# First tile of x on another queue, a warming matmul moved, and state-space groups stepped in pairs, in a hybrid decoder layer

## Chip, cores and metric

The kernel runs on one core of one Trainium2 chip. The time is device microseconds of one execution; the kernel before was run three times and has 1466.87 us as its median.

## The reference

One decoder layer on 256 tokens of width 2048, in float32. Cut to what matters here:

```python
u    = rmsnorm(x, norm_mix_pre)
proj = u @ w_in                       # columns: z | x, B, C | dt | q | k | v
xbc  = silu(causal_depthwise_conv(xbc, conv_w, conv_b))
dt   = softplus(dt_raw + dt_bias);  a = -exp(a_log)
# Mamba-2, 8 groups of 4 heads of 64, state 128, two chunks of 128 tokens:
y    = (cb * decay_in) @ xdt  +  exp(a_cs) * (C @ states)  +  d_skip * x
yg   = y * silu(z);  yg = yg * rsqrt(mean(yg * yg, over the group) + EPS)
y_ssm = yg * ssm_norm_w
# 16 heads of dilated attention, three dilations mixed by softmax
h = x + rmsnorm(concat(y_ssm, y_att) @ w_out)
h = h + rmsnorm(relu(rmsnorm(h) @ w_up)**2 @ w_down)
```

Nearly all of the work is in the four products with `w_in`, `w_out`, `w_up` and `w_down`.

## The kernel before

Every weight is split into two parts, `hi` and `lo` (ScalarE rounds `hi` from the loaded tile `raw`, line 144; VectorE takes `lo = raw - hi`, line 145), and so are the activations (`ua`, `ub`, `uc` hold u; `sh`, `sl` and others what follows). A product is the sum of three of the four part products. A step is one tile of 256 rows by 512 columns of a weight: one load (line 158, from SP's queue, four `raw` buffers), one `hi`, one `lo` (five buffers each) and 16 or 12 matmuls. A block of 512 columns has eight steps. `gemm_features` (lines 468 and 471) gives a block with features on the partitions, `gemm_tokens` (`row_tile`, lines 323 to 325) one with tokens on the partitions.

The state-space part runs block by block: for each half, a features block for B and one for C, then twice a features block for x (`conv_block`, with the convolution on VectorE, lines 735 and 737) and a tokens block for the gate z (`gate_block`). Each x block holds two groups. Their own small work is a generator, `ssd_group`, that stands in the queue `waiting`. After each step of a block, `pump` takes the generator at the head, lets it write its program up to the next `yield` and puts it back at the end. So the small matmuls of the groups lie between the steps of later blocks, and with two groups waiting they take turns. The parts of a group are, by what TensorE does:

- line 752: the group's rows of `acs` are loaded into `bc` on ScalarE's queue (two buffers); lines 757 to 768: C times B, and transposes of B and x;
- lines 784 to 786: decays in `bc` (VectorE, and exp on ScalarE); line 789: the state (`st`);
- line 793: C times the state, which becomes `yo` (line 795); line 801: the decays in `bc` times x, 8 small matmuls; then `yg` (804, 806), its squares (810, ScalarE), their mean `rm` (138), the inverse root `gr` (139, GpSimd) and the scaling (814);
- line 821: four transposes of `yg`, split into `sh` and `sl`.

The small products go to PSUM tiles `ps`, of which there are two. Within an engine the order is set by a scheduler from the order and the priorities in which the program is written; weights have priority (`high_priority`), and an engine then takes its instructions strictly in that order.

The first block (`first_block`, priority and order by hand) loads x and the first weights in turn on SP's queue, while TensorE does matmuls of ones (`warm`), the transpose of the norm's weight `pre` and the transposes of the first tile of x (`turn_x`, line 549).

Of the kernel before, what the change touches and what calls it, by code (L numbers as in the profile page):

```python
# [44 lines left out]
BUFS = 5  # L45
RAWS = 4
LAG_DOWN = 3
WARM = 6
STAY = 4
SUMS = 10  # L50
FINE = 6
FIRST = 3
UP_SEVENS = (1, 3, 4, 6)
V_SEVENS = (1, 3, 5, 6)
QK_SEVENS = (1, 3, 5)
# [22 lines left out]
def hymba_layer(ctx: ExitStack, tc: tile.TileContext, x, norm_mix_pre, w_in, conv_w, conv_b, dt_bias, a_log,  # L78
                d_skip, ssm_norm_w, w_out, norm_mix_post, norm_mlp_pre, w_up, w_down, norm_mlp_post,
                consts, out):  # L80
    nc = tc.nc
    w_in, w_out, w_up, w_down = w_in[0], w_out[0], w_up[0], w_down[0]
    xt = x[0].rearrange("(t p) d -> p t d", p=P)
# [48 lines left out]
    def psmall():  # L132
        return psm.tile([P, NB], F32, name="ps")
# [170 lines left out]
    waiting = deque()  # L304
# [213 lines left out]
        for _ in range(n):  # L518
            nc.tensor.matmul(p[:, 0:P], ones, ones, start=True, stop=True)

    def load_x(k0):
        cs = slice(k0 * P, (k0 + KB) * P)
        nc.sync.dma_start(xs0[:, :, cs], xt[:, :, cs])

    def load_parameters():
        for r, src in enumerate((norm_mlp_pre, ssm_norm_w)):
# [16 lines left out]
    def turn_x(k0):  # L543

        q = [psmall() for _ in range(KB)] if k0 % (2 * KB) else spare
        for f in range(KB):
            for t in range(NT):
                ks = slice((k0 + f) * P, (k0 + f + 1) * P)
                nc.tensor.transpose(q[f][:, t * P:(t + 1) * P], xs0[:, t, ks], ident)
        return q  # L550
# [9 lines left out]
    def first_block():  # L560
        acc = features()
        raws = {}

        def load(k0):
            raws[k0] = fetch(w_in, k0, COL_B, step=1 if k0 < FINE else KB)

        def part(k0, hi, lo, js):
            split(hi[:, js], lo[:, js], raws[k0][:, js])

        load_x(0)  # L570
        load(0)
        load_x(KB)
        load(KB)
        p = psmall()
        nc.tensor.transpose(p[:, 0:16], pre, ident[0:16, 0:16])
        nc.vector.tensor_copy(w_pre, p[:, 0:16])
        q = turn_x(0)
        warm(STAY)
        hi, lo = parts()
        for f in range(KB):  # L580
            split_x(0, q, f)
            part(0, hi, lo, slice(f, f + 1))
        for k0 in range(0, NK, KB):
            k1, k2 = k0 + KB, k0 + 2 * KB
            if k2 < NK:
                load_x(k2)
                load(k2)
            elif k2 == NK:
                load_parameters()
            products(acc, hi, lo, k0, [(f, 0) for f in range(4)])  # L590
            if k1 < NK:
                q = turn_x(k1)
            products(acc, hi, lo, k0, [(f, 1) for f in range(4)])
            if k1 == NK:
                break
            hi, lo = parts()
            if k1 >= FINE:
                part(k1, hi, lo, slice(0, KB))
            for f in range(KB):
                behind[:] = split_x(k1, q, f)  # L600
                if k1 < FINE:
                    part(k1, hi, lo, slice(f, f + 1))
            if k0 >= 4:
                squares(k0 // KB - 2)
        return acc

    nc.scalar.activation(rstd, half[:, 0:NT], AF.Copy)
    with tc.high_priority(offset=2 * AHEAD), tc.manual_schedule():
        nc.sync.dma_start(ident, consts[:, 0:P])
        nc.scalar.dma_start(pre, norm_mix_pre[0].rearrange("(k p) -> k p", p=P))  # L610
        warm(WARM)
        first = first_block()
# [135 lines left out]
    def ssd_group(sp, g, bT, cT, xT, z):  # L748

        hs = slice(HPG * g, HPG * (g + 1))  # L750
        bc = sp.tile([P, HPG, S], F32, name="bc")
        nc.scalar.dma_start(bc, acs_d[hs].partition_broadcast(P))

        p = psmall()
        for c in range(NT):
            cs = slice(c * P, (c + 1) * P)
            nc.tensor.matmul(p[:, cs], bT[:, cs], cT[:, cs], start=True, stop=True)
        nc.tensor.transpose(p[:, S:S + P], bT[:, 0:P], ident)
        cbm = sp.tile([P, NT, P], F32, name="cbm")
        nc.vector.tensor_tensor(cbm, p[:, :S].rearrange("p (c i) -> p c i", c=NT),  # L760
                                triu[:, None, :].to_broadcast([P, NT, P]), op=ALU.mult)
        bn = sp.tile([P, P], F32, name="bn")
        nc.vector.tensor_copy(bn, p[:, S:S + P])

        p = psmall().rearrange("p (c f) -> p c f", c=NT)
        for c in range(NT):
            for f in range(2):
                nc.tensor.transpose(p[:, c, f * P:(f + 1) * P], xT[:, f, c * P:(c + 1) * P], ident)
        xs = sp.tile([P, NT, HPG, HD], F32, name="xs")
        nc.scalar.activation(xs.rearrange("p c r d -> p c (r d)"), p, AF.Copy)  # L770
        xdt = sp.tile([P, NT, HPG, HD], F32, name="xdt")
        for c in range(NT):
            nc.vector.tensor_tensor(xdt[:, c], xs[:, c], dt[:, c, hs, None].to_broadcast([P, HPG, HD]), op=ALU.mult)
        xdd = sp.tile([P, HPG, HD], F32, name="xdd")
        nc.gpsimd.tensor_tensor(xdd, xdt[:, 0], toend[:, hs, None].to_broadcast([P, HPG, HD]), op=ALU.mult)
        for c in range(NT):
            nc.gpsimd.tensor_tensor(xs[:, c], xs[:, c], skip_b[:, hs, None].to_broadcast([P, HPG, HD]), op=ALU.mult)
        yield

        for c in range(NT):  # L780
            m = bc[:, :, c * P:(c + 1) * P]
            for r in range(HPG):
                h = HPG * g + r
                nc.vector.tensor_scalar(m[:, r], m[:, r], acs[:, c, h:h + 1], 0.0, op0=ALU.subtract, op1=ALU.min)
            nc.scalar.activation(m, m, AF.Exp)
            nc.vector.tensor_tensor(m, m, cbm[:, c, None, :].to_broadcast([P, HPG, P]), op=ALU.mult)

        p = psmall()
        nc.tensor.matmul(p[:, :S], bn, xdd.rearrange("p r d -> p (r d)"), start=True, stop=True)
        st = sp.tile([P, HPG * HD], F32, name="st")  # L790
        nc.vector.tensor_copy(st, p[:, :S])
        yield
        nc.tensor.matmul(p[:, S:], cT[:, P:], st, start=True, stop=True)
        yo = sp.tile([P, HPG, HD], F32, name="yo")
        nc.vector.tensor_tensor(yo, p[:, S:].rearrange("p (r d) -> p r d", r=HPG),
                                eacs[:, hs, None].to_broadcast([P, HPG, HD]), op=ALU.mult)
        nc.gpsimd.tensor_tensor(xs[:, 1], xs[:, 1], yo, op=ALU.add)
        p = psmall().rearrange("p (c r d) -> p c r d", c=NT, r=HPG)
        for c in range(NT):
            for r in range(HPG):  # L800
                nc.tensor.matmul(p[:, c, r], bc[:, r, c * P:(c + 1) * P], xdt[:, c, r], start=True, stop=True)

        yg = sp.tile([P, NT, HPG * HD], F32, name="yg")
        nc.vector.tensor_tensor(yg, p.rearrange("p c r d -> p c (r d)"), xs.rearrange("p c r d -> p c (r d)"),
                                op=ALU.add)
        nc.vector.tensor_tensor(yg, yg, z, op=ALU.mult)
        gs = sp.tile([P, NT], F32, name="gs")
        for c in range(NT):
            junk = sp.tile([P, HPG * HD], BF16, name="gj")
            nc.scalar.activation(junk, yg[:, c], AF.Square, accum_out=gs[:, c:c + 1])  # L810
        gr = sp.tile([P, NT], F32, name="gr")
        rsqrt_mean(gr, gs, HPG * HD)
        for c in range(NT):
            nc.vector.tensor_scalar(yg[:, c], yg[:, c], gr[:, c:c + 1], None, op0=ALU.mult)
        yield
        yield
        yield
        p = psmall().rearrange("p (f s) -> p f s", f=2)
        for f in range(2):
            for c in range(NT):  # L820
                nc.tensor.transpose(p[:, f, c * P:(c + 1) * P], yg[:, c, f * P:(f + 1) * P], ident)
        for f in range(2):
            k = 2 * g + f
            split(sh[:, k], sl[:, k], p[:, f], w_ssm[:, k:k + 1])

    sp = ssd.enter_context(tc.tile_pool(name="sp", bufs=2, side="right", reuse_waits="tile"))
    for hb in range(2):
        bT = conv_block(COL_B + hb * NB, 16 + 4 * hb, first if hb == 0 else None)
        if hb == 0:
            waiting.append(steps())  # L830
        cT = conv_block(COL_C + hb * NB, 24 + 4 * hb)
        for xb in (2 * hb, 2 * hb + 1):
            xT = conv_block(COL_X + xb * NB, 4 * xb)
            z = gate_block(COL_Z + xb * NB)
            for j in range(2):
                g = 2 * xb + j
                waiting.append(ssd_group(sp, g, bT[:, g % 4], cT[:, g % 4], xT[:, 2 * j:2 * j + 2],
                                         z[:, :, j * 256:(j + 1) * 256]))


    def attention(ap, h, qT, kT, v):
# [608 lines left out]
```

## Time and profile before

| | us |
|---|---|
| three runs | 1466.87, 1465.23, 1468.87 |
| profiled execution, its own time | 1465.38 |
| its span, first to last instruction | 1463.5 |
| TensorE busy | 1452.7 |
| VectorE busy | 1255.5 |
| ScalarE busy | 888.0 |
| GpSimd busy | 143.3 |

In the profile PE is TensorE's matmuls and PEld its weight loads, DVE is VectorE, ACT ScalarE, POOL GpSimd and SP the engine that only issues transfers; a q behind a name is the engine's queue. `out<-in` are the names of tiles. Busy shares say how long an engine had something in work; the waits, the chain and the timeline say what it stood still for. A float32 matmul appears as two passes (x16 for the eight of line 801).

### The profile page before, as it was taken

The page shows a single profiled execution, that of the slowest core. Times are in us where ns is not written, and L with a number is a line of the kernel's source. Part 1 is how long each engine was busy: PE and PEld are TensorE (multiplying, and loading weights), DVE is VectorE, ACT ScalarE, POOL GpSimd, SP SyncE. Part 2 cuts the span into 40 slices and gives each one's busy share as a digit, 9 for nine tenths or more (in the row PEclk, how much of TensorE's full clock was granted, in tenths as well). Part 3 has the DMA queues.
Part 4 walks back from the last instruction along what each step waited for, and adds up shares of the span by engine and source line. Part 5 has one row for each costly group of instructions (what it writes and reads, how often), then busy time and mean ns, then how long its engine had stood idle before and what let it go on. Part 6 is the DMA issues. An engine that isn't in the chain of part 4 may idle for free.

```text
span 1463.5 us, 20269 instructions
## 1 busy us (share of the span) xinstructions
PE 1452.7 (99%) x7129; PEld 1223.1 (84%) x7129; DVE 1255.5 (86%) x1864; ACT 888.0 (61%) x1214; POOL 143.3 (10%) x208
## 2 busy tenths in 40 slices
PE   9999999999999999999999999999999999999998
PEld 8888888888888888888887888888878888888886
DVE  6798797898887686689979999988888999999987
ACT  7475675465566556555557677655455766765653
POOL 0003100212010000000100011000111111101000
PEclk9999999999999999999999999999999999999999
DMA  8666666566886486688867798777788988778963
GB/s 272 209 203 181 179 186 190 176 181 177 234 234 205 133 243 200 194 263 252 252 192 242 207 309 238 218 216 225 224 235 285 266 244 247 208 240 250 311 205 115
DMA packets 168022, 323.53 MB, mean 221 GB/s; under 512 B 15168, under 2 KB 18096, under 8 KB 167920
## 3 DMA queue, kind: packets, MB, share of 16 engines
q1 hardware_dynamic: 144576, 272.50, 59.0%
q0 software_dynamic: 15616, 36.19, 12.3%
q10 hardware_dynamic: 7728, 13.54, 2.7%
q8 instruction: 56, 0.92, 0.2%
q14 instruction: 46, 0.38, 0.1%
HBM read 317.96 MB, written 40.41 MB: 245 GB/s over the span
## 4 chain that ended last, share of the span: by engine, by line
PE 94%; DVE 3%; DMA 2%; ACT 1%; issue 1%; SPq 0%; POOL 0%; DVEq 0%; ACTq 0%
PE acc L468 15%; PE acc L324 12%; PE acc L323 12%; PE acc L325 11%; PE acc L471 8%; PE acc L407 5%; PE acc L406 5%; PE acc L408 5%; PE ps L324 3%; PE ps L325 3%; PE ps L323 3%; PE ps L406 2%; PE ps L408 2%; PE ps L407 2%; DVE lo L145 1%; DMA raw<-pair 1%
## 5 line engine op out<-in xcount | busy, mean ns | idle before, releaser
L144 ACT ACTIVATE hi<-raw 128x1024 fp32r<-128x1024 f32 (+1 forms) x418 | 437.7, 1051 | 292.1 <-PE acc L325 94.2
L145 DVE TENSOR_TENSOR lo<-raw,hi 128x1024 fp32r<-128x1024 f32 (+1 forms) x418 | 508.7, 1220 | 99.6 <-ACT hi L144 94.4
L468 PE MATMUL acc<-ua,hi 128*128 128x512 f32 x600 | 163.5, 401 | 0.1
L468 PEld LDWEIGHTS acc<-ua,hi 128*128 128x128 f32 x600 | 105.7, 189 | 17.1 <-ACT hi L144 0.2
L144 ACT ACTIVATE hi<-e 128x1024 fp32r<-128x1024 f32 x61 | 64.8, 1063 | 80.9 <-DVE e L247 74.3
L323 PE MATMUL acc<-hi,ua 128*128 128x512 f32 x248 | 98.5, 397 | 0.0
L324 PE MATMUL acc<-lo,ua 128*128 128x512 f32 x248 | 96.8, 390 | 0.0
L471 PEld LDWEIGHTS acc<-ua,lo 128*128 128x128 f32 x600 | 88.2, 189 | 10.3
L325 PE MATMUL acc<-hi,ua 128*128 128x512 f32 x248 | 96.7, 390 | 0.0
L471 PE MATMUL acc<-ua,lo 128*128 128x256 f32 x600 | 90.8, 281 | 0.0
L323 PE MATMUL acc<-hi,sh 128*128 128x512 f32 x224 | 88.4, 395 | 0.0
L324 PE MATMUL acc<-lo,sh 128*128 128x512 f32 x224 | 87.3, 390 | 0.8 <-DVE lo L145 0.8
L325 PE MATMUL acc<-hi,sl 128*128 128x512 f32 x224 | 87.3, 390 | 0.0
L145 DVE TENSOR_TENSOR lo<-e,hi 128x1024 fp32r<-128x1024 f32 x61 | 74.3, 1217 | 0.0
L468 PE MATMUL acc<-uc,hi 128*128 128x512 f32 x240 | 68.4, 397 | 0.0
L406 PE MATMUL acc<-hi,ah 128*128 128x512 f32 x166 | 64.6, 389 | 0.0
L407 PE MATMUL acc<-lo,ah 128*128 128x512 f32 x166 | 64.6, 389 | 0.0
L408 PE MATMUL acc<-hi,al 128*128 128x512 f32 x166 | 64.6, 389 | 0.0
L145 DVE TENSOR_TENSOR lo<-uc,hi 128x1024 fp32r<-128x1024 f32 x38 | 46.2, 1221 | 15.2 <-ACT hi L144 15.0
L325 PE MATMUL acc<-hi,al 128*128 128x512 f32 x148 | 57.6, 389 | 0.0
L323 PE MATMUL acc<-hi,ah 128*128 128x512 f32 x148 | 57.6, 389 | 0.0
L324 PE MATMUL acc<-lo,ah 128*128 128x512 f32 x148 | 57.6, 389 | 0.0
(526 smaller groups left out, 3413.9 us busy)
## 6 DMA issues: line engine op xcount, KB each, us to landing
raw<-in_w_in_dram SPq DMA_DIRECT2D x181, 512.0 KB, 4.1
raw<-in_w_down_dram SPq DMA_DIRECT2D x79, 512.0 KB, 5.3
raw<-in_w_up_dram SPq DMA_DIRECT2D x65, 512.0 KB, 4.7
raw<-in_w_out_dram SPq DMA_DIRECT2D x39, 512.0 KB, 5.0
pair<-in_w_up_dram POOLq DMA_DIRECT2D x56, 256.0 KB, 5.3
raw<-pair SPq DMA_DIRECT2D x50, 256.0 KB, 4.3
pair<-in_w_down_dram POOLq DMA_DIRECT2D x46, 256.0 KB, 6.6
ha<-in_w_up_dram SPq DMA_DIRECT2D x20, 512.0 KB, 5.7
```

Of the source, the lines that this page charges most:

```text
L144: return (nc.scalar.activation(hi, src, AF.Copy), nc.vector.tensor_tensor(lo, src, hi.bitcast(F32), op=ALU.subtract))
L145: nc.vector.tensor_tensor(lo, src, hi.bitcast(F32), op=ALU.subtract))
L323: nc.tensor.matmul(dst, a_h[:, r, ts], hi[:, j], start=begin and j == 0, stop=False)
L324: nc.tensor.matmul(dst, a_h[:, r, ts], lo[:, j], start=False, stop=False)
L325: product[t] = nc.tensor.matmul(dst, a_l[:, r, ts], hi[:, j], start=False, stop=end and j == KB - 1)
L406: nc.tensor.matmul(dst, a_h, hi[:, j], start=own and first, stop=False)
L407: nc.tensor.matmul(dst, a_h, lo[:, j], start=False, stop=False)
L408: nc.tensor.matmul(dst, a_l, hi[:, j], start=False, stop=own and last)
L468: nc.tensor.matmul(acc[f], hi[:, j, f * P:(f + 1) * P], u(k0 + j), start=k0 + j == 0, stop=False, skip_group_check=True)
L471: nc.tensor.matmul(acc[f][:, 0], lo[:, j, f * P:(f + 1) * P], u(k0 + j)[:, 0], start=False, stop=k0 + j == NK - 1, skip_group_check=True)
```

## The change

Three edits. The load of x's first tile leaves SP's queue and becomes the first transfer on ScalarE's, ahead of `pre`. Of the six warming matmuls at the start one is done later, behind `pre`'s transpose. And the two groups of a block no longer take turns: `two_groups` steps both, with rests between the steps after `PACE`, and `ssd_group` has a new `yield` between line 793 and line 801 and two fewer ahead of the last transposes.

```diff
-WARM = 6
+WARM = 5
+PACE = (3, 1, 4, 0)
...
-    def load_x(k0):
+    def load_x(k0, queue=nc.sync):
         cs = slice(k0 * P, (k0 + KB) * P)
-        nc.sync.dma_start(xs0[:, :, cs], xt[:, :, cs])
+        queue.dma_start(xs0[:, :, cs], xt[:, :, cs])
...
-        load_x(0)
         load(0)
         load_x(KB)
         load(KB)
         p = psmall()
         nc.tensor.transpose(p[:, 0:16], pre, ident[0:16, 0:16])
         nc.vector.tensor_copy(w_pre, p[:, 0:16])
+        warm(1)
         q = turn_x(0)
         warm(STAY)
...
         nc.sync.dma_start(ident, consts[:, 0:P])
+        load_x(0, nc.scalar)
         nc.scalar.dma_start(pre, norm_mix_pre[0].rearrange("(k p) -> k p", p=P))
         warm(WARM)
...
         nc.gpsimd.tensor_tensor(xs[:, 1], xs[:, 1], yo, op=ALU.add)
+        yield
         p = psmall().rearrange("p (c r d) -> p c r d", c=NT, r=HPG)
...
         yield
-        yield
-        yield
         p = psmall().rearrange("p (f s) -> p f s", f=2)
...
+    def two_groups(a, b):
+
+        next(a)
+        yield
+        next(b)
+        yield
+        yield
+        for rest in PACE:
+            for g in (a, b):
+                next(g, None)
+            for _ in range(rest):
+                yield
...
-            for j in range(2):
-                g = 2 * xb + j
-                waiting.append(ssd_group(sp, g, bT[:, g % 4], cT[:, g % 4], xT[:, 2 * j:2 * j + 2],
-                                         z[:, :, j * 256:(j + 1) * 256]))
+            waiting.append(two_groups(*(ssd_group(sp, g, bT[:, g % 4], cT[:, g % 4], xT[:, 2 * j:2 * j + 2],
+                                                  z[:, :, j * 256:(j + 1) * 256])
+                                        for j, g in enumerate((2 * xb, 2 * xb + 1)))))
```

What it moves. The program's lines are numbered up to three higher after the change (line 468 becomes 469, 801 becomes 804, 814 becomes 817, 821 becomes 822). First the start of the program on SP's queue, before, where `xs` is x, `raw` a weight tile and `ident` the identity for transposes:

```order
L609 DMA ident<-in_consts_dram 128x128
L523 DMA xs_106<-in_x_dram 128x2x256
L158 DMA raw<-in_w_in_dram 128x512 x2
L523 DMA xs_106<-in_x_dram 128x2x256
L158 DMA raw<-in_w_in_dram 128x512 x2
```

On ScalarE, before:

```order
L610 DMA pre<-in_norm_mix_pre_dram 16x128
L607 ACT_TABLE_LOAD
L607 ACTIVATE rstd<-half 128x2
L146 ACTIVATE ua<-acc,par 128x256
L144 ACTIVATE hi<-raw 128x512
```

On SP after the change:

```order
L610 DMA ident<-in_consts_dram 128x128
L159 DMA raw<-in_w_in_dram 128x512 x2
L524 DMA xs_106<-in_x_dram 128x2x256
L159 DMA raw<-in_w_in_dram 128x512 x2
L524 DMA xs_106<-in_x_dram 128x2x256
```

And on ScalarE after it:

```order
L524 DMA xs_106<-in_x_dram 128x2x256
L612 DMA pre<-in_norm_mix_pre_dram 16x128
L608 ACT_TABLE_LOAD
L608 ACTIVATE rstd<-half 128x2
L147 ACTIVATE ua<-acc,par 128x256
```

The first tile of x is one place ahead of `pre` on ScalarE, and on SP every weight and later tile of x has moved up by one.

Second, TensorE in the x block behind the first pair of groups, before, from the first group's line 793 to the second group's line 801 (`st` is the state, `bc` the decays, `xdt` x times dt):

```order
L793 MATMUL ps<-st,cT 128x256
L468 MATMUL acc<-ub,hi 128x512 x7
L801 MATMUL ps<-xdt,bc 128x64 x8
L468 MATMUL acc<-ub,hi 128x512
L471 MATMUL acc<-ub,lo 128x256 x8
L793 MATMUL ps<-st,cT 128x256
L801 MATMUL ps<-xdt,bc 128x64 x8
```

The same place after the change:

```order
L795 MATMUL ps<-st,cT 128x256 x2
L469 MATMUL acc<-uc,hi 128x512 x2
L472 MATMUL acc<-uc,lo 128x256 x2
L469 MATMUL acc<-uc,hi 128x512 x2
L472 MATMUL acc<-uc,lo 128x256 x2
L469 MATMUL acc<-uc,hi 128x512 x2
L472 MATMUL acc<-uc,lo 128x256 x2
L469 MATMUL acc<-uc,hi 128x512 x2
L472 MATMUL acc<-uc,lo 128x256 x2
L804 MATMUL ps<-xdt,bc 128x64 x16
```

Both groups' line 793 now stand together, both groups' line 801 a whole step behind them, at the end of the block. The transposes of line 821, ahead of the change five steps behind the second line 801 and one step apart, stand together four steps behind it.

Third, VectorE from there on, before:

```order
L795 TENSOR_TENSOR yo<-ps,eacs 128x256
L804 TENSOR_TENSOR yg<-ps,xs 128x512
L806 TENSOR_TENSOR yg<-yg,tk 128x512
L795 TENSOR_TENSOR yo<-ps,eacs 128x256
L804 TENSOR_TENSOR yg<-ps,xs 128x512
L145 TENSOR_TENSOR lo<-raw,hi 128x1024
L138 TENSOR_SCALAR rm<-gs 128x2
L806 TENSOR_TENSOR yg<-yg,tk 128x512
L814 TENSOR_SCALAR yg<-yg,gr 128x256 x2
```

And after the change, from the second group's `yg`:

```order
L807 TENSOR_TENSOR yg<-ps,xs 128x512 x2
L809 TENSOR_TENSOR yg<-yg,tk 128x512 x2
L739 TENSOR_SCALAR cT<-pad,cw,cT 128x256 x3
L146 TENSOR_TENSOR lo<-raw,hi 128x1024
L139 TENSOR_SCALAR rm<-gs 128x2 x2
L739 TENSOR_SCALAR cT<-pad,cw,cT 128x256
L817 TENSOR_SCALAR yg<-yg,gr 128x256 x3
L146 TENSOR_TENSOR lo<-raw,hi 128x1024
L817 TENSOR_SCALAR yg<-yg,gr 128x256
```

The work of both groups is written side by side, ahead of it stands the convolution of the next block (`cT`, `pad`), and the last piece of the second group's scaling is one `lo` behind the others.

## The prediction

> **What bounds the kernel now.** I read the page's busy table first, then TensorE's own waits, then the timeline of the two places that are edited.
>
> ```profile
> PE 1452.7 (99%) x7129; PEld 1223.1 (84%) x7129; DVE 1255.5 (86%) x1864; ACT 888.0 (61%) x1214; POOL 143.3 (10%) x208
> PE ps L1318 <- ACT dg L1317: 2.0, 1, 2.0
> PE ps L519 <- DVE half L508: 1.1, 1, 1.1
> PE ps L1099 <- DVE ha L1090: 1.0, 1, 1.0
> PE ps L848 <- DVE mx L856: 0.9, 1, 0.9
> PE acc L324 <- DVE lo L145: 0.8, 1, 0.8
> ```
>
> TensorE is busy 1452.7 of 1463.5 us. The second group of rows (engine, line, what it waited for: us in total, times, longest) shows that no single wait is over 2.0 us and that none of the five longest has a line of the state-space groups (L757 to L821) in it: they are the start (L519), the first attention heads (L848), the turn to the MLP (L1099), one weight (L324) and the end (L1318). So time can only be won in this kernel where TensorE stands still or does extra work, and lost where it is made to wait. The first edit is at the start, where it does stand still; the second is in a stretch where it hardly does.
>
> The start, from the timeline of all engines (start us, duration, engine, line, operation; in brackets the idle time before it and what ended it; "q" is the engine's own issuing of a transfer):
>
> ```profile
> 0.74 0.42 ACTq L610 DMA_DIRECT2D pre<-in_norm_mix_pre_dram  x1
> 0.75 0.39 SPq L609 DMA_DIRECT2D ident<-in_consts_dram  x1
> 1.06 2.93 PE L519 MATMUL ps<-ones 128*128 128x128 f32 x12 [1.06 <-DVE half L508]
> 1.19 0.42 SPq L523 DMA_DIRECT2D xs<-in_x_dram  x1
> 1.20 1.28 ACT L607 ACT_TABLE_LOAD   x1 [1.20 <-PEq L1438]
> 1.66 0.93 SPq L158 DMA_DIRECT2D raw<-in_w_in_dram  x2
> ...
> 4.26 0.42 PEld L549 LDWEIGHTS acc<-ident,xs 128*128 128x128 f32 x4 [0.21 <-DMA xs<-in_x_dram]
> 4.75 1.06 PE L519 MATMUL ps<-ones 128*128 128x128 f32 x8
> 5.17 0.63 ACT L144 ACTIVATE hi<-raw 128x512 fp32r<-128x512 f32 x1
> 5.87 1.18 PE L468 MATMUL acc<-ua,hi 128*128 128x512 f32 x4
> ...
> 7.61 0.42 PEld L549 LDWEIGHTS ps<-ident,xs 128*128 128x128 f32 x4 [0.28 <-DMA xs<-in_x_dram]
> ```
>
> The first product (L468) begins at 5.87. Ahead of it are warming matmuls, the transposes of the first tile of x (4.26, ended by the transfer of x), the split of that tile, and the first half of the first weight (hi at 5.17). The second tile of x lets TensorE go on only at 7.61. The chain of waits says the same, and the tile's own view and the list of transfers give the flights:
>
> ```profile
> 2.64 4.92 DMA xs<-in_x_dram
> DMA to landing us min/median/max: 3.0/5.9/6.8
> pre<-in_norm_mix_pre_dram ACTq DMA_DIRECT2D x1, 8.0 KB, 1.9
> 8.00:16.00 8.00, 8.00 (x51) 7.03 (x49) 6.28 (x12) 6.30 (x14) 0.00 (x0) 1.00 1.06 390
> ```
>
> The first row is the longest transfer on the chain: the second tile of x, issued at 2.64, 4.92 us in flight. The first tile took 3.0 us (the least of the second row), pre took 1.9 (last column of the third). The last row is a stretch of the windows view (length, busy time of TensorE, weight loads, and so on): from 8 to 16 us TensorE is busy for all 8.00.
>
> **The change, part by part.** First tile of x on ScalarE's queue. SP no longer spends 1.66 - 1.19 = 0.47 us on it, so the first weight, the second tile and all that follow are issued up to 0.47 us earlier; the first tile itself is issued where pre was, at 0.74 instead of 1.19, 0.45 us earlier. pre goes out one issue (0.42) later. ScalarE's table load, queued behind both issues, slides from 1.20 to about 1.6 and ends near 2.9; ScalarE's first work on x stands behind the transposes (4.26), so this costs nothing while they end after 3. If first and second tile land 0.45 earlier, TensorE could go on at 3.8 and 7.1. But it also has its warming matmuls to do: with one fewer ahead of pre they end about 2 x 2.93/12 = 0.49 earlier, near 3.5, then come pre's transpose and the moved matmul (another 0.49), so that x's transposes start at about 4.1 to 4.2: a gain of 0.1 to 0.2 there, with no less work on TensorE. At the second tile the products of the first (half a step, about 1.4 us by the steps shown below) end near 7.2 and x has landed near 7.1, against 7.61: a gain of about 0.35. From 8 us on TensorE has no gap, so what is won here stays. Bounds: 0.47 won (all of the issue time) to some loss, if pre, now behind 256 KB of x in the same queue, comes late: not before 1.16 + 1.9 = 3.1, and at the latest about when x has, 0.74 + 3.0 = 3.8 or shortly after. Then TensorE stands still from 3.5 to 3.9 and the gain at the first tile is gone, while that at the second stays. I take -0.35, near the row of the second tile, because that is what TensorE waits for last. [...]
>
> State-space groups in pairs. Eight groups, four pairs. TensorE's stretch with the first two groups, and two plain steps of a features block elsewhere (eight products with hi of 128x512, then eight with lo) for comparison:
>
> ```profile
> 115.72 0.59 PE L789 MATMUL ps<-xdd,bn 128*128 128x256 f32 x2
> ...
> 122.17 0.60 PE L793 MATMUL ps<-st,cT 128*128 128x256 f32 x2
> ...
> 124.22 1.94 PE L801 MATMUL ps<-xdt,bc 128*128 128x64 f32 x16
> ...
> 127.24 0.60 PE L793 MATMUL ps<-st,cT 128*128 128x256 f32 x2
> ...
> 129.37 2.10 PE L468 MATMUL acc<-uc,hi 128*128 128x512 f32 x8
> 35.24 1.84 PE acc L468 x8
> 38.03 1.84 PE acc L468 x8
> ```
>
> A plain step takes 38.03 - 35.24 = 2.79 us. From 115.72 to 122.17 TensorE does two steps and two visits of L789, so one such visit of two passes costs (6.45 - 5.58)/2 = 0.43. L793, of the same shape, costs the same; the visit of L793 and L801 at 127.24 takes 129.37 - 127.24 = 2.13, so L801's 16 passes take 1.70. The first group's L801, which stands alone in the stream at 124.22, costs 127.24 - 122.17 - 2.79 - 0.43 = 1.85: 0.15 more. That is the most that a visit of its own costs beyond its passes, and part of it is a wait. Before, a pair breaks into the stream nine times, now six (preparations twice; L789, L793, L801, L821 once each for both): 12 visits fewer in four pairs, so between 0 and 12 x 0.15 = 1.8 us. The other thing to save is a wait:
>
> ```profile
> PEld ps L801 <- DVE yo L795: 0.7, 4, 0.2
> L144 ACT ACTIVATE hi<-raw 128x1024 fp32r<-128x1024 f32 x14 | 14.8, 1055 | 16.5 <-PE acc L468 11.4 <-PE acc L325 3.3 <-ACT cT L739 0.9
> ```
>
> The second group's L801 waited for yo (L795) to free the small PSUM buffer, 0.7 us in four times, on the weight loads. The new break between L793 and L801 takes that away, since a whole step lies between. It lies beside the passes of L793 (TensorE's own waits have no such row), so of these two terms (0 to 1.8 and 0 to 0.7) I take -0.2 together, near the lower end.
>
> What hides the rest: the work of VectorE and ScalarE is the same and only bunched. Those engines run ahead of TensorE: of 16.5 us that ScalarE was idle before its 14 hi's of 105 to 150 us, 11.4 + 3.3 was ended by TensorE, that is, by a buffer of the five coming free. The cover is thus up to four steps, 4 x 2.79 = 11 us. In pairs ScalarE's two loads of bc (L752) stand together and wait for both groups' L801: the second ends 2 x 1.76 = 3.5 us after the first began. The hi's behind them wait for buffers that TensorE frees still later, after its next step (3.5 + 2.8). Nothing is lost there unless the cover goes below zero. A new deadline does appear: L821 of both groups now comes four steps after both L801. What must be done by then:
>
> ```profile
> 129.67 0.69 DVE L804 TENSOR_TENSOR yg<-ps,xs 128x512 f32<-128x512 f32 x1 [1.38 <-PE ps L801]
> 131.48 0.68 DVE L806 TENSOR_TENSOR yg<-yg,tk 128x512 f32<-128x512 f32 x1
> 136.02 0.15 DVE L138 TENSOR_SCALAR rm<-gs 128x2 f32<-128x2 f32 x1
> L139 POOL TENSOR_TENSOR gr<-rm,half x8: 702/1078/2200, 131.7 to 336.3; 128x2 f32<-128x2 f32 x8
> 138.49 0.61 DVE L814 TENSOR_SCALAR yg<-yg,gr 128x256 f32<-128x256 f32 x2 [0.25 <-POOL gr L139]
> ...
> 136.69 1.21 DVE L145 TENSOR_TENSOR lo<-raw,hi 128x1024 fp32r<-128x1024 f32 x1
> 143.79 0.48 DVE L737 SCALAR_TENSOR_TENSOR cT<-pad,cw,cT 128x256 f32<-128x256 f32 x1
> ...
> 146.47 0.60 PE L821 MATMUL ps<-ident,yg 128*128 128x128 f32 x4
> ```
>
> Before, the second group had from 129.4 to 146.47, 17 us, and used 10 of them (to 139.1). In the new order VectorE runs, after the second L801: L804 0.69, L806 twice 1.36, three of the convolution's L737 1.44, a lo 1.21, the two rm 0.3, an L737 0.48; then GpSimd the two gr, and the second group's L814 in two halves with a lo between, 0.31 + 1.21 + 0.31. With gr at 1.08 (the median of the L139 row) that is 5.5 + 2.2 + 1.8 = 9.5 us; with 2.20 (the longest) 11.7. The time there is: four steps and the first group's four transposes (0.60 in the row), 11.2 + 0.6 = 11.8. So it fits by 2.3 us at the median and by 0.1 at the longest. I take no cost and keep the failure as a rival.
>
> The sum against the profiled execution (1465.38 us; its span is 1463.5 and 1.9 lies around it): 1465.38 - 0.35 - 0.2 = 1464.8. The median of the three runs, 1466.87, lies 1.49 above it, so the forecast is 1466.87 - 0.55 = 1466.3. Nothing in the change touches what comes after 360 us but the order of VectorE and ScalarE in the first heads, where L848 waited 0.9; the rows ahead of that wait stay as they are.
>
> **The rivals.**
>
> Slower: late transposes. If gr runs long and one of ScalarE's hi's (which waits for TensorE) gets between the squares, about 1.05 more, the chain is 11.7 + 1.05 = 12.8 against 11.8, and L821 waits 1.0 us in each of four pairs; with a second hi in between, 2.05: 4 to 8 us, so about 1472. For it: the longest gr is twice the median. Against it: 2.3 us of room at the median, and VectorE busy for 1255.5 of 1463.5 us only. It decides where L814 of the second group ends after TensorE's four steps. Chance 0.08.
>
> Slower: TensorE's clock comes late. The warming rows show it: 12 passes in 2.93 us, 0.24 each, at first and 8 in 1.06, 0.13, later; full speed is there by 4.75. If TensorE stands still for pre at 3.5 to 3.9, full speed may come later, and the work of 4.3 to 7.6, some 3.3 us, stretch to up to twice; some of that lies beside the flight of the second tile, so I take about two thirds: +2.0, 1468.9. [...] Chance 0.07.
>
> Nothing at the start: the DMA engines are the limit, x lands no earlier, and only the -0.2 is left: 1466.7. For it: all transfers share the engines. Against: at 0.74 only ident (64 KB by its tile) is issued beside it. Chance 0.13.
>
> The main case keeps 0.72.
>
> **How the numbers follow.** Runs of the kernel before spread from 1465.23 to 1468.87, so about 0.3%, 4.4 us, is what a measurement can tell from no change. The main case by the bounds of its terms is 1466.87 - 2.97 (0.47 + 1.8 + 0.7) = 1463.9 to 1466.87; with about half of the spread of runs below the median (-1.64) and all of it above (+2.00) 1463.0 to 1468.9. The clock rival's 1468.9 and some of its spread bring the upper end to 1470.5; the late transposes at 1472 are left out. Faster than 1462.5 needs half as much again as all the terms at their far ends: 0.06, for what I have not seen. Slower than 1471.3 needs the late transposes, 0.08, and a little for the unseen: 0.1. The rest, 0.84, is within.
>
> **What would show it.** In the changed profile: the first L468 at 5.6 to 5.8 and the second transposes of x at about 7.2; no wait at L821 (its new line L822) or at L801 (L804) in TensorE's waits; steps of 2.79 between the visits; the wait of 0.7 for yo gone. Late transposes would show as waits of TensorE for yg near 145 us and at the three later pairs; a late clock as passes of 0.2 us after 4.3. The prediction is wrong if TensorE's busy time or the sum of its waits differs by more than 2 us.

## The result, and the profile after

The changed kernel takes 1468.54 us (median of 22 runs, 1466.04 to 1475.19) against 1465.89 (22 runs, 1461.95 to 1470.56): the ratio is 1.0023, with a 95% interval of 1.0014 to 1.0031, so 2.1 to 4.5 us slower. The forecast was 1466.3, that is 0.55 faster, which it took as too little to be told from no change. The measured time lies in the range given there, but the step has the other sign. The profiled execution took 1468.20, its span 1466.4.

The page's first row, and the two rows of TensorE's waits that are new in the edited places:

```profile
PE 1454.0 (99%) x7129; PEld 1225.3 (84%) x7129; DVE 1251.9 (85%) x1864; ACT 885.8 (60%) x1212; POOL 142.4 (10%) x208
```

```profile
PE ps L575 <- DMA pre<-in_norm_mix_pre_dram: 1.8, 1, 1.8
...
PE ps L791 <- POOL xdd L777: 0.4, 1, 0.4
```

TensorE's busy time grew by 1.3 us, although it runs the same 7129 passes. The two waits are 1.8 us for the transfer of pre (L575) and 0.4 for GpSimd's xdd (L791). The wait for mx (L848 before, L861 now; lines behind the state-space groups stand 13 higher after the change, not three) is gone. The start, from the timeline:

```profile
0.74 0.47 ACTq L524 DMA_DIRECT2D xs<-in_x_dram  x1
1.06 2.50 PE L520 MATMUL ps<-ones 128*128 128x128 f32 x10 [1.06 <-DVE half L509]
1.24 0.48 ACTq L612 DMA_DIRECT2D pre<-in_norm_mix_pre_dram  x1
...
5.39 0.26 PE L575 MATMUL ps<-ident,pre 16*128 16x16 f32 x1 [1.83 <-DMA pre<-in_norm_mix_pre_dram]
5.58 0.80 PE L520 MATMUL ps<-ones 128*128 128x128 f32 x2
...
6.16 1.06 PE L550 MATMUL acc<-ident,xs 128*128 128x128 f32 x4
...
7.02 1.92 PE L520 MATMUL ps<-ones 128*128 128x128 f32 x8
...
8.58 2.05 PE L469 MATMUL acc<-ua,hi 128*128 128x512 f32 x4
```

After 10 warming passes TensorE has nothing to do from 3.56 to 5.39; pre's transpose, two warming passes and x's transposes follow, and the first product begins at 8.58 in place of 5.87, 2.71 later. Only 5.39 - 3.92 = 1.47 of that is the later pre. Another 0.43 lies between pre's transpose and those of x (6.16 - 5.39 in place of 4.26 - 3.92), where the moved warming matmul now stands (two passes, 0.80). The rest, 0.81 (6.16 to 8.58 in place of 4.26 to 5.87), is pace: the 8 warming passes behind x's transposes (7.02) take 1.92 in place of 1.06, the transposes (6.16) 1.06 in place of 0.66. TensorE still runs slowly here, 0.24 us a pass where it was 0.13, and the trace's records of the granted clock agree: the first of full speed (1.00) stands at 10.57, before the change at 3.91, and none stands ahead of it. These two records last 1454.08 us before and 1450.66 after, 426 and 425 times 3.413 us; a stretch of 3.413 us, counted from such a record, is called a window here. The transfers, from the chain of waits and from the list of transfers up to 12 us (last column: us from issue to landing):

```profile
1.24 4.01 DMA pre<-in_norm_mix_pre_dram
```

```profile
xs<-in_x_dram ACTq DMA_DIRECT2D x1, 256.0 KB, 3.6
ident<-in_consts_dram SPq DMA_DIRECT2D x1, 64.0 KB, 3.0
pre<-in_norm_mix_pre_dram ACTq DMA_DIRECT2D x1, 8.0 KB, 4.0
```

pre lands at 5.25 (before: 0.74 + 1.9, about 2.6). x's first tile, issued 0.45 earlier, lands at 4.38 against 4.22: later. ident takes 3.0 in place of 2.1. Why, is in the packets moved from 3 to 4 us by each queue (q1 is SP's, q10 ScalarE's; packets, MB, share of the 16 engines), first before, then after:

```profile
q1 hardware_dynamic: 203, 0.27, 97.2%
```

```profile
q1 hardware_dynamic: 101, 0.16, 57.8%
q10 hardware_dynamic: 173, 0.16, 47.1%
```

Before, one queue had nearly all of the engines (97.2%), and what it carried landed in the order of issue: ident at 2.85, x at 4.22, the second tile of x at 7.56. After, two queues move 0.16 MB each in this microsecond, 57.8 and 47.1% of the same 16 engines. By the packets of the two traces, x's 256 start from 2.10 to 4.04 (before, from 2.29 to 3.82), the weights, in the other queue, from 2.99 on (3.17), and the last of ident's begins at 3.37 (2.29). The 16 packets with pre's data start from 3.98 to 4.72, when x's in the same queue are all but through.

From 38 us on the lag is constant. The same product (eight passes) begins at 38.03 before (shown in the prediction) and at 41.21 here. From the chains of waits, after, and then of before the row that answers to the last:

```profile
41.21 1.84 PE acc L469 x8
44.00 1.84 PE acc L469 x8
...
355.52 1.84 PE acc L469 x8
```

```profile
351.95 1.84 PE acc L468 x8
```

41.21 - 38.03 = 3.18 us lost at the start; 355.52 - 351.95 = 3.57 after the last pair. So the four pairs did not win 0.2 but lost 0.39. In the plain steps ahead of the first pair the lag is 3.20, behind the third 2.88, behind the fourth 3.57. That last step, +0.69, is the wait for xdd, which holds TensorE's weight loads for 0.8 us, once (the matmuls behind them have 0.43 of it). First the row of the weight loads' waits, then the timeline of VectorE, GpSimd and TensorE:

```profile
PEld ps L791 <- POOL xdd L777: 0.8, 1, 0.8
```

```profile
317.83 1.80 POOL L777 TENSOR_TENSOR xdd<-xdt,toend 128x256 f32<-128x256 f32 x1 [23.25 <-DVE xdt L775]
317.94 1.22 DVE L146 TENSOR_TENSOR lo<-raw,hi 128x1024 fp32r<-128x1024 f32 x1
...
319.59 4.15 POOL L779 TENSOR_TENSOR xs<-xs,skip_b 128x256 f32<-128x256 f32 x2
319.61 0.74 DVE L775 TENSOR_TENSOR xdt<-xs,dt 128x256 f32<-128x256 f32 x2
320.28 1.28 DVE L788 TENSOR_TENSOR bc<-bc,cbm 128x512 f32<-128x512 f32 x2
321.49 1.21 DVE L146 TENSOR_TENSOR lo<-raw,hi 128x1024 fp32r<-128x1024 f32 x1
323.70 0.61 POOL L777 TENSOR_TENSOR xdd<-xdt,toend 128x256 f32<-128x256 f32 x1
...
324.37 0.70 PE L791 MATMUL ps<-xdd,bn 128*128 128x256 f32 x2 [0.43 <-POOL xdd L777]
```

xdd of the second group (L777 at 323.70) stands in GpSimd's queue behind two products of the first group with skip_b (L779), which take 4.15 us together; one of them 3.58:

```profile
L779 POOL TENSOR_TENSOR xs<-xs,skip_b x16: 606/1057/3577, 116.3 to 325.8; 128x256 f32<-128x256 f32 x16
```

The least of the row is 0.61. The first group's xdd already took 1.80 beside a lo (317.83 and 317.94). The long product lasted for as long as VectorE ran one operation with two inputs after another (L775, L788, L146, five of them from 319.61 to 322.70) and ended 0.5 us after that row broke (319.59 + 3.58 = 323.17). The one behind it, to 323.74, took the least time, 0.61, and VectorE's next such operation, another lo, began only at 323.72. So in this trace the long product and VectorE's row fall together; why GpSimd takes longer there, no run shows.

The rival of the prediction that I feared in this place did not come. From the timeline:

```profile
138.38 0.69 DVE L807 TENSOR_TENSOR yg<-ps,xs 128x512 f32<-128x512 f32 x1 [0.49 <-PE ps L804]
...
146.73 0.35 DVE L817 TENSOR_SCALAR yg<-yg,gr 128x256 f32<-128x256 f32 x1
...
149.10 1.04 PE L822 MATMUL ps<-ident,yg 128*128 128x128 f32 x8
```

From the second group's L807 (138.38) to the end of its L817 (146.73 + 0.35) VectorE and GpSimd needed 8.7 us, and TensorE's transposes (L822) began 2.0 us later without a wait.

### The profile page after: what moved, and what is told of

Read it like the earlier page. It is cut to its first block, busy times and chain, and to the rows that moved or that the text cites. A ratio compares the mean times of both kernels' runs of the same rounds, so it can differ in the third digit from the quotient of the medians.

```text
span 1466.4 us, 20271 instructions
## 1 busy us (share of the span) xinstructions
PE 1454.0 (99%) x7129; PEld 1225.3 (84%) x7129; DVE 1251.9 (85%) x1864; ACT 885.8 (60%) x1212; POOL 142.4 (10%) x208
## 4 chain that ended last, share of the span: by engine, by line
PE 90%; DVE 4%; DMA 3%; issue 1%; ACT 1%; POOL 0%; ACTq 0%; SPq 0%; DVEq 0%; POOLq 0%
PE acc L469 15%; PE acc L324 11%; PE acc L326 11%; PE acc L325 11%; PE acc L472 8%; PE acc L407 5%; PE acc L408 5%; PE acc L409 5%; PE ps L325 3%; PE ps L326 3%; PE ps L324 3%; PE ps L407 2%; PE ps L408 2%; PE ps L409 2%; DVE lo L146 2%; DMA raw<-pair 2%
## 5 line engine op out<-in xcount | busy, mean ns | idle before, releaser
L146 DVE TENSOR_TENSOR lo<-raw,hi 128x1024 fp32r<-128x1024 f32 (+1 forms) x418 | 507.8, 1219 | 112.7 <-ACT hi L145 108.7
L146 DVE TENSOR_TENSOR lo<-e,hi 128x1024 fp32r<-128x1024 f32 x61 | 74.3, 1218 | 0.0
L146 DVE TENSOR_TENSOR lo<-uc,hi 128x1024 fp32r<-128x1024 f32 x38 | 46.2, 1221 | 14.9 <-ACT hi L145 14.7
```

The source lines that it names most:

```text
L146: nc.vector.tensor_tensor(lo, src, hi.bitcast(F32), op=ALU.subtract))
```

## The experiments

All nine are set against the kernel before. "Lag" is how much later than there the same product begins: the ones at 38.03 and at 351.95. "Clock" is the trace's first record of full speed. These columns are one profiled execution of each kernel. The ratios come with their 95% intervals, of 12 runs each (22 of the changed kernel); where an interval reaches 1 or less, the times alone do not tell the kernel from the one before, and the argument goes by the traces.

```
kernel        pre    x      first    clock   lag at  lag at  ratio to the kernel before
              lands  lands  product          38 us   352 us
before        2.62   4.22   5.87     3.91    0       0       1
changed       5.25   4.38   8.58     10.57   3.18    3.57    1.0023 [1.0014, 1.0031]
start_only    5.51   4.71   8.84     9.59    2.87    2.92    1.0017 [1.0003, 1.0030]
pairs_only    2.73   4.46   6.26     4.83    -0.11   0.26    1.0004 [0.9993, 1.0016]
pre_first     2.64   5.65   8.18     10.55   2.96    3.35    1.0009 [0.9998, 1.0020]
warm12        5.35   4.53   7.71     4.70    1.39    1.82    1.0013 [1.0000, 1.0026]
pause         2.66   3.91   6.43     8.63    1.09    1.13    1.0013 [1.0001, 1.0025]
warm_moved    2.57   4.06   6.60     6.47    0.30    0.34    0.9993 [0.9980, 1.0006]
pre_on_sp     4.12   3.94   7.45     9.18    1.90    2.31    1.0009 [0.9997, 1.0021]
xdd_vector    2.61   4.10   5.80     4.27    0.04    -0.29   0.9996 [0.9986, 1.0006]
x_first       4.95   4.78   7.74     8.69    1.89    1.55    1.0015 [1.0005, 1.0026]
```

**start_only** and **pairs_only**: each half of the change alone. The edits are those of the diff above.

> The kernel before with the start's edit alone (x's first tile on ScalarE's queue, five warming matmuls ahead of pre and one behind). Theory A (the whole loss is the start: pre stands behind 256 KB of x in ScalarE's queue, lands at 5.25 instead of 2.62, TensorE stands still from 3.56 to 5.39 and the full clock comes at 10.57 instead of 3.91): the first L468 begins near 8.6, TensorE's lag behind the kernel before is 3.2 us from about 30 us on and stays so to the end, time +3.2 us or a little less if in other runs the clock comes a window earlier: +2 to +3.2. Theory B (the start's 3.2 is half accident of one profiled run, and the pairs cost the rest): first L468 near 7 to 7.5, time +1 to +1.5.

> The changed kernel with the start of the kernel before. Theory A: first L469 at 5.87, full clock near 3.9; the four pairs win 0.1 to 0.2 us each in TensorE's time, the wait for xdd (0.7 us at the fourth pair) is an accident of one execution or stays, and the first heads win 1.2 because they come at another place against VectorE's queue: time -0.3 to -1.5 us. Theory B: pairs cost: +1 to +1.5.

The start alone lags by 2.87 and keeps it to 352 us (2.92), and it is slower by 0.4 to 4.4 us: Theory A; the 7 to 7.5 of Theory B for the first product is far off the 8.84. Theory A for the pairs came out only in part: the first product stands at 6.26 in place of 5.87, the full clock at 4.83 in place of 3.9, and the 1.2 us at the first heads were not won (TensorE waits 1.6 for mx, before 0.9). The pairs alone win 0.31 over three pairs and lose 0.69 in the fourth, so they cost 0.37 between the two columns. The wait for xdd is no accident of one execution: it is there in every profile with pairs in which GpSimd computes xdd (0.4 to 0.5 us), as here in pairs_only.

```profile
PE ps L790 <- POOL xdd L776: 0.4, 1, 0.4
```

By time the pairs alone are between 1.0 faster and 2.3 slower, which cannot tell 0.37 from nothing. So A is right on the start, and its "accident, or stays" for the pairs is decided: stays.

**pre_first**: the two issues on ScalarE's queue in the other order.

```
-        load_x(0, nc.scalar)
         nc.scalar.dma_start(pre, norm_mix_pre[0].rearrange("(k p) -> k p", p=P))
+        load_x(0, nc.scalar)
```

> The changed kernel with the two issues on ScalarE's queue in the other order: pre at 0.74, x's first tile behind it near 1.2 (as late as in the kernel before, but SP's queue still free of it). Theory A (the order inside the one queue is what made pre late): pre lands at 2.6 to 2.9, the transposes of x run at 4.2 to 4.5, the full clock comes near 3.9, first L469 at 5.8 to 6.0, the time is that of the pairs alone: 3 us below the changed kernel. Theory B (x beside SP's transfers on a second queue is what delays pre, whatever the order): pre still lands after 4 and at least half of the loss stays.

Neither as written. pre lands at 2.64, as A has it, and yet 2.96 of the lag stays, because x now comes late:

```profile
PE acc L550 <- DMA xs<-in_x_dram: 1.2, 1, 1.2
```

```profile
xs<-in_x_dram ACTq DMA_DIRECT2D x1, 256.0 KB, 4.5
pre<-in_norm_mix_pre_dram ACTq DMA_DIRECT2D x1, 8.0 KB, 1.9
```

x is issued at 1.19, when it was issued before the change, but on a queue of its own, and takes 4.5 us in place of 3.0. So what made x early before was not when it was issued. What fits is that the weights stood behind it in the same queue and now run beside it; x_first below shows that this alone is not enough. TensorE now waits for x instead of pre, and the clock is just as late. By time this kernel is between 0.3 us faster and 2.9 slower than the one before, so the runs do not show whether all of the 2.96 stays in every execution. I took as the new theory that a pause of TensorE, for whatever transfer, costs the clock.

**warm12**: no pause, with pre as late.

```
-WARM = 5
+WARM = 12
```

> The changed kernel with 12 warming matmuls (24 passes) ahead of pre in place of 5: pre is as late as in the changed kernel, but TensorE has no pause before it. Theory C (the late clock is a part of the loss by itself: a pause of 1.8 us costs two windows): passes of 0.11 from about 3.9 on, the full clock at 3.9, pre's transpose near 5.4, the transposes of x near 5.7, first L469 at about 7.2 to 7.4: 1.3 us of the 2.7 come back, and the products from 8 to 10.6 at full speed bring another 0.5: about 1.5 to 1.8 us below the changed kernel. Theory D (the clock comes late for another reason, and only pre's lateness matters): full clock again after 7, first L469 at 8.4 to 8.7, time as the changed kernel.

```profile
1.06 4.67 PE L520 MATMUL ps<-ones 128*128 128x128 f32 x24 [1.06 <-DVE half L509]
...
6.58 1.06 PE L520 MATMUL ps<-ones 128*128 128x128 f32 x8
7.71 1.16 PE L469 MATMUL acc<-ua,hi 128*128 128x512 f32 x4
```

Theory C: with pre at 5.35 and TensorE warming until 5.73, the 8 passes behind x's transposes take 1.06 again, full speed is recorded at 4.70, and the lag is 1.39 in place of 3.18. So in these two executions 1.79 of the start's loss is the clock and up to 1.39 the late transfers: the longer warming itself has some 0.2 of that, since pre's transpose begins 0.31 after pre has landed, in the changed kernel 0.14. The times do not show this split: warm12 is 0 to 3.8 us slower than before, the changed kernel 2.1 to 4.5.

**pause**: a pause with no change of any transfer, in the kernel before.

```
-WARM = 6
+WARM = 3
```

> The kernel before with 3 warming matmuls (6 passes) in place of 6 ahead of pre, and no other change: all transfers are issued as before, x's first tile lands near 4.2 to 4.5, and TensorE stands still from about 2.9 to 4.3. Theory C (a pause in the first microseconds costs the clock one or two windows of about 3.4 us each): full clock after 7, the transposes of x take 1.06 in place of 0.66, the 8 warming passes 1.9 in place of 1.06, first L468 near 7.0 (+1.1), lag 1.2 to 2 us from 30 us on. Theory D (only late transfers matter): first L468 at 5.9 to 6.2, lag below 0.4.

```profile
1.06 1.65 PE L519 MATMUL ps<-ones 128*128 128x128 f32 x6 [1.06 <-DVE half L508]
...
3.96 1.11 PE L549 MATMUL acc<-ident,xs 128*128 128x128 f32 x4 [0.74 <-DMA xs<-in_x_dram]
...
4.87 1.92 PE L519 MATMUL ps<-ones 128*128 128x128 f32 x8
...
6.43 2.05 PE L468 MATMUL acc<-ua,hi 128*128 128x512 f32 x4
```

Theory C again, at its lower edge: x even landed early here, at 3.91, but the transposes take 1.11, the warming passes 1.92, the four products 2.05 (1.18 before), and 1.09 us are lost for three warming matmuls left out. D falls.

**warm_moved**: the second half of the start's edit alone.

```
-WARM = 6
+WARM = 5
...
+        warm(1)
         q = turn_x(0)
```

> The kernel before with the second half of the start's edit alone: five warming matmuls ahead of pre, one behind it, x on SP's queue as before. Theory A (the moved matmul is harmless; the queue is the cause): pre's transpose near 3.5, no pause over 0.3 us before x's transposes at 4.2 to 4.5, full clock between 3.9 and 4.9, first L468 at 5.8 to 6.3, lag at 30 us between -0.2 and +0.3, time within 0.1% of the kernel before. Theory B (the moved matmul alone unsettles the clock): full clock after 7, lag 1.2 to 2.

Closer to A than to B, but at A's edge: no pause, a lag of 0.30, and full speed at 6.47, later than A allows and earlier than B has it. Here TensorE worked on from 1.06 without a break over 0.2 us. Why full speed came later than at 3.91, no run shows; the section on the hardware has TensorE's idle time ahead of it. The time, 2.9 faster to 0.9 slower, shows no loss.

**pre_on_sp**: pre on SP's queue behind ident, x alone on ScalarE's.

```
         nc.sync.dma_start(ident, consts[:, 0:P])
+        nc.sync.dma_start(pre, norm_mix_pre[0].rearrange("(k p) -> k p", p=P))
         load_x(0, nc.scalar)
-        nc.scalar.dma_start(pre, norm_mix_pre[0].rearrange("(k p) -> k p", p=P))
```

> The changed kernel with pre issued on SP's queue, right behind ident, so that nothing stands ahead of it but ident and x has ScalarE's queue to itself. Theory A (pre behind x in one queue is all that is wrong with the start): pre lands at 3 to 4, x's first tile at 4.4 to 4.7 as in the changed kernel, L550 at 4.5 to 4.8, a pause of at most 0.5 us, full clock by 4.9, first L469 at 6.0 to 6.4, lag at 30 us of 0 to 0.4. Theory E (two queues share the transfer engines, so that x on its own queue is not sooner, and the short pause still costs the clock): first L469 near 7, lag at 30 us of 1 to 2.5. No theory expects a lag below -0.3.

Theory E: pre still takes 2.9 us (4.12), x is there at 3.94, and with 0.7 us of pause before pre's transpose full speed comes at 9.18. The lag is 1.90. Taking pre out from behind x mends 1.28 of the 3.18 in these executions; by time the kernel is 0.4 faster to 3.1 slower than the one before.

**xdd_vector**: pairs_only, with xdd on VectorE.

```
-        nc.gpsimd.tensor_tensor(xdd, xdt[:, 0], toend[:, hs, None].to_broadcast([P, HPG, HD]), op=ALU.mult)
+        nc.vector.tensor_tensor(xdd, xdt[:, 0], toend[:, hs, None].to_broadcast([P, HPG, HD]), op=ALU.mult)
```

> The pairs with the start of the kernel before (pairs_only), and xdd (0.41 us, eight times) computed by VectorE in place of GpSimd. Theory P (the 0.69 us that the fourth pair loses is TensorE waiting for GpSimd, whose xdd of the second group stands behind the first group's two products with skip_b, one of which VectorE's two-input operations hold up to 3.58 us): the wait for xdd goes, one product with skip_b on GpSimd at the fourth pair is still over 2 us, the lag at 340 us goes from +0.26 to -0.2 to -0.5. Theory Q (the pair itself is too dense there and another wait takes its place): lag at 340 us stays over 0.1.

```profile
L778 POOL TENSOR_TENSOR xs<-xs,skip_b x16: 608/788/3912, 112.4 to 322.2; 128x256 f32<-128x256 f32 x16
```

```profile
351.66 1.84 PE acc L469 x8
```

Theory P: no wait for xdd is left, a product with skip_b still takes 3.91 (that VectorE's operations hold it was my guess from the one trace above, and no run tested it), and the lag goes from 0.04 to -0.29 over all four pairs. So pairs win 0.33 us, somewhat more than the 0.2 that the prediction took, where nothing waits on GpSimd; x_first, with the same xdd, wins 0.34 over them (1.89 to 1.55). It is the best version with pairs, and by its ratio it cannot be told from the kernel before (2.1 faster to 0.9 slower).

**x_first**: xdd_vector, with x the first issue of SP's queue.

```
-        load_x(0)
         load(0)
...
-        nc.sync.dma_start(ident, consts[:, 0:P])
+        load_x(0)
+        nc.scalar.dma_start(ident, consts[:, 0:P])
         nc.scalar.dma_start(pre, norm_mix_pre[0].rearrange("(k p) -> k p", p=P))
```

> The pairs with xdd on VectorE (xdd_vector), and the first issues dealt otherwise: x's first tile is the first issue on SP's queue (0.75 in place of 1.18), with the weights behind it in the same queue, and ident and pre go out on ScalarE's queue. Theory F (x is early when it leads the queue that the weights follow in, and small transfers beside it cost little): x lands at 3.5 to 4.0, ident at 3.0 to 3.6, pre by 4.0, first product 5.5 to 5.9, lag at 30 us of -0.5 to 0, so a start no worse than before and the pairs' -0.3 on top: time 0.3 to 0.8 us below the kernel before. Theory G (two queues share the transfer engines evenly, so ident and pre are late beside x): pre after 4.2, a pause of TensorE before it, and where that spoils a window of the clock a lag at 30 us of 0.5 to 2.

```profile
ident<-in_consts_dram ACTq DMA_DIRECT2D x1, 64.0 KB, 3.4
pre<-in_norm_mix_pre_dram ACTq DMA_DIRECT2D x1, 8.0 KB, 3.7
```

Theory G. Everything comes later than before the change: ident (3.4 in place of 2.1 us), pre (3.7 in place of 1.9) and even x itself, issued 0.44 earlier and landed at 4.78. TensorE waits 1.1 us for pre, full speed comes at 8.69, and it is slower by 0.7 to 3.8 us. Here x led its queue and the weights stood behind it, and still x took 4.0 us with 72 KB beside it on the other queue; why so much, no run shows.

## Why the prediction was wrong, step by step

- **x 0.45 earlier by an issue 0.45 earlier** failed first. I carried the flight of 3.0 us over to another queue. It belonged to a place in a queue: in five profiles with x on SP's queue behind ident it landed at 3.91 to 4.46; on ScalarE's queue at 3.94 to 5.65, never clearly sooner. The 0.47 of issue time was a bound from above; what spoke against the edit, that a second queue's packets take engine time beside the first's (from 3 to 4 us 47.1% and 57.8%, where one queue had 97.2), I had not weighed. The rival "Nothing at the start" had the shared engines in it, but priced them as no gain, not as a loss.
- **pre "at the latest about when x has, 3.8 or shortly after"** failed by 1.4 us: 5.25. I saw that pre stood behind x in its queue, but not that x, and pre behind it, would share the engines with the weights.
- **The start's term**, -0.35, was thus of the wrong sign: +3.18, of which, by warm12, up to 1.39 are late transfers and 1.79 the clock.
- **The rival "clock comes late"** had the mechanism, a pause for pre, and nearly the size (+2.0 taken, 1.79 by warm12). That its 1468.9 lies so near the measured 1468.54 is luck, since it counted from a slower median of the kernel before (1466.87 of three runs, 1465.89 of 22) and left the late transfers out. What failed was its chance, 0.07: the pause was put at 0.4 us, where it was 1.8, and the time of pre, on which it hung, was not the uncertain end of a range but the likeliest case.
- **The second tile at 7.1** could not come into play: by then TensorE had not begun its first product. Its sum did not hold either. It took 1.4 us for the products of the first tile; in the timeline of before they run from 5.87 to the end of L471 (row below), 7.53, which is 1.66. Begun 0.1 to 0.2 earlier, they end at about 7.4, so by these rows some 0.2 was there to win against the 7.61, not 0.35. That tile's flight of 4.92 is the longest of the start alone, not of the whole chain (6.27 at 1058.86); nothing hung on that.

```profile
6.89 0.64 PE L471 MATMUL acc<-ua,lo 128*128 128x256 f32 x4
```

- **The gain of the pairs**, -0.2, was about right where no wait came in between: -0.32 over the first three pairs, -0.33 over four in xdd_vector. The wait of 0.7 for yo is gone, as forecast, and plain steps stayed at 2.79 (41.21 to 44.00).
- **"What hides the rest"** was checked for ScalarE and VectorE, not for GpSimd. Its queue in the pair, two products between the two xdd, cost 0.69 net. That GpSimd's operations run up to twice their median was in the rows of the prediction (gr 1.08 and 2.20); I put that risk on gr, where pairing made it smaller (0.95 at most now).
- **Late transposes** at L822 did not come, with 2.0 us to spare against the 2.3 worked out.
- **The sum**: 3.18 + 0.39 = 3.57 at 352 us. From there to the end of the span the lag of the nine experiments moves by -1.6 to +3.2 us more (of the changed kernel by -0.7), with the wait at the first heads and the MLP's start, whatever was edited; the runs' 3.4 (2.1 to 4.5) is about what the two terms make.
- **The sign of being wrong**, busy time or waits off by more than 2 us, did not show it: TensorE's busy time grew by 1.3 us and its listed waits by 1.4 (6.4 to 7.8), each below 2, while the span grew by 2.9. The slower passes count as busy (the 8 behind x's transposes 1.92 us in place of 1.06), so the two belong in one sum.

## What to carry to other kernels

The flight of the first transfers was here a matter of their place among the others: moving x's first tile to an idle queue put what stood behind it beside it, and the small load that followed it there came 2.6 us later. So ask first which transfer TensorE waits for with the least slack, and what will run beside it. No order of the first issues tried here beat the one before. A step that takes work in pairs must be followed on every queue that holds work of both, GpSimd's too (0.69 us lost here at its xdd).

## What the runs showed of the hardware

In the six profiles with a pause of TensorE of 0.7 to 2.1 us in the first microseconds full speed came at 8.6 to 10.6 us, in the five with none over 0.3 us at 3.9 to 6.5. Full speed lasted 426 windows of 3.413 us before the change (1454.08 us), 425 after it (1450.66), and in pause a first stretch of 447.15, which is 131.

TensorE's idle time in the windows ahead of full speed can be added up in the eleven traces, counted back from each first record of full speed (the ends of matmuls are modelled in them; what lies ahead of the span counted as idle). In the last window it was zero in eight of them, 0.20 and 0.30 in xdd_vector and pairs_only, and 0.57 in the kernel before. In the window ahead of that one it was at least 0.69 (pre_on_sp; 1.20 in pre_first, 1.64 in the changed kernel). So in these starts full speed came behind a window with at most 0.57 us of idle time, and not behind the one ahead of it, with 0.69 or more. In warm_moved, where there was no pause, that earlier window began at 6.47 - 6.83 = -0.36 and was idle for 1.42, all of it ahead of TensorE's first matmul at 1.06. In the changed kernel the window that began at 0.33 was idle for 0.73 before TensorE began and for 0.19 in the pause, the next, from 3.75, for 1.64, all in the pause. So only the second of these two has all of its idle time in the pause. No run shows what sets where the windows begin, or whether that differs between executions of one kernel.

Full speed was also lost far from the start. At the first heads TensorE waits for mx, in these eleven profiles from nothing to 3.1 us, and no run shows what sets it. In three profiles (pause, pre_on_sp, x_first) the clock fell there for one window (in pause to 0.50). Counted in the same way, the windows ahead of these three losses were idle for 3.13, 1.94 and 2.62 us; in start_only and xdd_vector, with 1.66 idle in one window, nothing was lost. So full speed was kept here with 1.66 us of idle time in a window, and at the start of pre_on_sp not reached with 0.69. From pause, the wait, and the windows view ahead of, in and behind that window (length, busy time of TensorE and the others, granted clock, share and rate of the transfers):

```profile
PE ps L848 <- DVE mx L856: 3.1, 1, 3.1
```

```profile
452.00:455.70 3.70, 0.57 (x5) 0.37 (x4) 2.75 (x7) 3.48 (x6) 0.00 (x0) 1.00 0.94 336
455.80:459.10 3.30, 3.30 (x10) 2.84 (x11) 1.52 (x11) 2.73 (x10) 0.00 (x0) 0.50 0.72 234
459.30:462.00 2.70, 2.70 (x17) 2.39 (x16) 2.28 (x8) 1.14 (x2) 0.00 (x0) 1.00 0.21 18
```

TensorE was busy 0.57 of 3.70 us, and then ran for one window, 3.41 us, at a clock of 0.50. The lag of pause went from 1.19 ahead of these heads to 5.05 behind them: 3.1 - 0.9 = 2.2 of the 3.9 is the longer wait, and the other 1.7, as an estimate, half of the 3.41 us at a clock of 0.50. In such an execution this place costs more than the pairs win (0.33).
